# A two-layer hybrid encoder block: layer B's turnings moved from TensorE to VectorE and DRAM, a fourth weight buffer, and a new order of layer B

## The chip, the cores and the metric

The kernel runs on one core of a Trainium2 chip. The metric is the device time of one execution in microseconds. Before the change it is 830.73 us, the median of three runs (830.43 to 831.87).

## What is computed

The input is one sequence of 512 tokens of width 1024, float32. Two layers follow each other, each of the form x + out(mix(norm(x))), with 16 heads of 64 channels.

```python
for i in range(DEPTH):                       # DEPTH = 2
    hn = rms_norm(x, norm_gain[i])
    y = mixer_a(hn, ...) if i % 2 == 0 else mixer_b(hn, ...)
    x = x + y

def mixer_b(hn, w_in, w_out, q_gain, k_gain, rpb):
    q, k, v, gate = split(hn @ w_in, 4)      # 1024 x 4096 weights
    q = rms_norm(q per head, q_gain) * 64 ** -0.5
    k = rms_norm(k per head, k_gain)
    # tokens stand on an 8 x 64 grid; the queries of a block of 16 columns see a slab of
    # 32 columns in all 8 rows, of which 16 columns a query are valid
    p = softmax(q @ k.T + bias)
    y = (p @ v) * silu(gate)
    return y @ w_out                         # 1024 x 1024 weights
```

Layer A (`mixer_a`) has three groups of dilated windows with their own queries, keys and values, merged by their softmax denominators, and takes the first 560 us or so of the trace; layer B is `mixer_b`.

## The kernel before, in words

**Products.** Every product with weights is made of three matmuls: an operand is split into a high part (in the type float32r) and a low part, and high x high, high x low and low x high are added up in PSUM. `mm3` issues the three. A wide product (`project`, line 251) has 512 output columns: for each of 8 slices of the contraction it visits four accumulators (`ps_acc`, four banks), 4 x 8 x 3 = 96 matmuls of 512 columns. A narrow one (`project_t`, line 276: a gate, or layer A's first values) has 24. The output product (`out_product`, line 988) has 8 slices times 8 output tiles times three.

**Weights.** `loads` (line 166) walks the weights in the order in which they are used, in pieces of up to 1024 columns (512 KB). `raws` (line 175) loads a piece on SP's queue into one of three buffers (`wraw`). `split` (line 128) makes the high part on ScalarE (line 132) and the low part (line 138), for two splits in five on GpSimd and for three on VectorE. Four splits are held ahead of TensorE.

**Order.** TensorE's order is the order in which the program is written. `run` (line 954) interleaves two generators: `main`, the products, and `side`, the attention work between them. A clock of estimated TensorE time counts each matmul as it is issued. `later_on` (line 235) puts a job at a later reading of this clock; a `yield "wait", key, delay` in `side` holds until a stamp is set and a delay has passed; a number yielded is a pause. The clock only sets the order of the program: on the chip an instruction waits for its operands. Instructions on the other engines are ordered by a scheduler at build time, but for those marked `keep_in_program_order`. SP's queue works its transfers off in order, and one that waits holds up those behind it.

**Layer B.** `B_PARTS` (line 38) is the order of its products: four wide Q/K products (each for two head pairs), two wide V products, eight gates; then the output product. Behind a Q/K product ScalarE empties each accumulator (line 493), GpSimd squares, VectorE reduces and norms per head (`head_norm`, line 296) and scales (line 313). `side_b(hc)` (line 1072) then handles a head pair: eight 128 x 128 transposes on TensorE (`transpose4`, line 326: four for the queries, four for the keys), copies out of PSUM that split them and bring the tokens into the order of the query blocks (lines 1087 to 1096), 24 score matmuls, a softmax per head and half (line 1131 on VectorE, 1141 and 725 on ScalarE). P^T then comes in one of two ways. For the first six pairs VectorE turns 32 x 32 blocks (`turner.put`, line 795), SP writes them to DRAM (line 804) and reads them back with the blocks exchanged (line 808). For the last two pairs `turn_p` (line 1147) transposes on TensorE, 14 transposes a pair, and VectorE copies them out. `weigh` multiplies with the values, `put_y` (line 727) multiplies with the gate and splits the result. The bias of a pair is read in six small transfers (`bias_b`, line 769). `residual` (line 1030) reads the rows that the output is added to, once all of P is used up.

Layer A moves its queries and keys of six head pairs in the way that the change brings to layer B: blocks of 32 x 32 turned by VectorE (`turn_raw`, line 525), a write to DRAM (line 655) and four reads (line 661).

Of the kernel before, what the change touches and what calls it, by code (L numbers as in the profile page):

```python
# [27 lines left out]
KT = 8  # L28
# [18 lines left out]
def tile_hybrid_encoder(  # L47
# [25 lines left out]

    mid_rc = lambda t: sb(t, 64, [[128, 3], [1, 8], [8, 16]])
    edge_rc = lambda t: sb(t, 0, [[448, 2], [1, 8], [8, 8]])
    mid_q = lambda t: sb(t, 0, [[128, 3], [16, 8], [1, 16]])
    edge_q = lambda t: sb(t, 384, [[64, 2], [8, 8], [1, 8]])
    mid_o = lambda t: sb(t, 64, [[128, 3], [16, 8], [1, 16]])
    edge_o = lambda t: sb(t, 0, [[448, 2], [8, 8], [1, 8]])
    mid_cr = lambda t: sb(t, 64, [[128, 3], [1, 16], [16, 8]])  # L80
    edge_cr = lambda t: sb(t, 0, [[448, 2], [1, 8], [8, 8]])
    mid_n = lambda t: sb(t, 64, [[128, 3], [8, 16], [1, 8]])
    edge_n = lambda t: sb(t, 0, [[448, 2], [8, 8], [1, 8]])

# [14 lines left out]
    gb_d = dr.tile([P, 248], F32, name="gb_d")  # L99

    v0 = [cp.tile([P, 4, P], F32, name=f"v0_{i}") for i in range(2)]
# [39 lines left out]
    def blocks():  # L141
# [10 lines left out]
        yield from outs(A_OUT)  # L152
# [22 lines left out]
    def raws():  # L175
        queue = []
        for src, cols, n in loads():
            raw = wp.tile([P, 1024], F32, tag="wraw", name="wraw", bufs=3)
# [5 lines left out]
            nc.sync.dma_start(dst, src)  # L184
            if behind:
                behind.pop()()
            queue.append((raw, cols, n))
            if len(queue) > 2:
                yield queue.pop(0)
        yield from queue  # L190

    def splits():
        queue = []
# [1176 lines left out]
```

## Time and profile before

| What | us |
|---|---|
| median of three runs | 830.73 |
| the profiled execution | 830.22 |
| its span, first to last instruction | 828.4 |
| TensorE busy | 822.4 |
| VectorE busy | 509.5 |
| ScalarE busy | 431.5 |
| GpSimd busy | 281.7 |

In the rows of the profile PE is TensorE's matmuls and PEld its weight loads, DVE is VectorE, ACT ScalarE, POOL GpSimd, and SPq the queue from which SyncE issues transfers. L215 is a line of the kernel's file; nearly all matmuls have line 215, that of the helper, and are told apart by tile: `acc` is a product, `log` scores, `o` weighing, `tp` a transpose. A row of a group ends with busy time, the mean duration of one in ns, and the idle time ahead of it with what ended it. A row of one line or tile shows the shortest, median and longest duration and the first and last start. A row in order of time begins with start and duration; a bracket is idle time ahead of it. In the row of a stretch each engine's busy time is followed by its count of instructions. Matmuls are pipelined: the distance between two starts, not the duration, is what one costs in a row.

### The profile page before, as it was taken

To read this page: it belongs to the slowest core of one execution; us is meant where nothing else is said; L and a number is where in the kernel's file an instruction comes from. 1 tells how busy PE (TensorE), PEld (TensorE's weight loads), DVE (VectorE), ACT (ScalarE), POOL (GpSimd) and SP (SyncE) were. 2 spreads that over 40 slices of the span, in tenths; PEclk is the share of its full clock that TensorE was granted. 3 is DMA by queue.
4 is the path that set the end of the run, shared out by engine and by line. 5 is a ranking of instruction groups with operands and counts; after the bars stand their busy time and mean duration, and the time that the engine had idled before them with its cause. 6 is when DMAs were issued, how large, how long until landed. Compare 5 with 4: busy or idle time off the path is not lost.

```text
span 828.4 us, 15450 instructions
## 1 busy us (share of the span) xinstructions
PE 822.4 (99%) x5616; PEld 667.2 (81%) x5616; DVE 509.5 (62%) x1356; ACT 431.5 (52%) x905; POOL 281.7 (34%) x424
## 2 busy tenths in 40 slices
PE   9999999999999999999999999999999999999998
PEld 7888888788788788788788787788878877877787
DVE  7374685673673673673684754556565778668653
ACT  7433753654554554553554554444366465774541
POOL 3352443343343343343333152021611625235211
PEclk9999999999999999999999999999999999999999
DMA  7487788779679669669675571373336546456323
GB/s 257 147 234 220 219 217 239 238 219 276 189 203 286 181 203 284 178 196 287 188 211 165 168 207 53 88 262 127 103 104 183 171 130 191 127 158 198 107 95 131
DMA packets 73324, 154.08 MB, mean 186 GB/s; under 512 B 6640, under 2 KB 32368, under 8 KB 73248
## 3 DMA queue, kind: packets, MB, share of 16 engines
q1 hardware_dynamic: 73104, 152.83, 61.8%
q8 instruction: 44, 0.72, 0.4%
q10 hardware_dynamic: 144, 0.26, 0.1%
q14 instruction: 32, 0.26, 0.1%
HBM read 117.04 MB, written 39.04 MB: 188 GB/s over the span
## 4 chain that ended last, share of the span: by engine, by line
PE 94%; ACT 2%; DVE 2%; issue 0%; DMA 0%; DVEq 0%; ACTq 0%
PE acc L215 82%; PE o L215 5%; PE log L215 5%; PE tp L219 2%; ACT p L1141 1%; ACT p L725 1%; DVE hn_l L405 1%; DMA x_all<-in_xt 0%; DVE rawq L313 0%; ACT rawq L493 0%; DVE wl L138 0%; DVE pt L1039 0%; ACT wh L132 0%; DVE p L1131 0%; PE pa L215 0%
## 5 line engine op out<-in xcount | busy, mean ns | idle before, releaser
L132 ACT CAST wh<-wraw 128x512 fp32r<-128x512 f32 (+1 forms) x259 | 158.4, 612 | 273.9 <-PE acc L215 255.5
L215 PE MATMUL acc<-wh,hn_h 128*128 128x512 f32 x704 | 280.0, 398 | 1.2 <-ACT hn_h L404 0.6
L215 PE MATMUL acc<-wh,hn_l 128*128 128x512 f32 x704 | 273.9, 390 | 0.0
L215 PE MATMUL acc<-wl,hn_h 128*128 128x512 f32 x704 | 273.8, 390 | 0.0
L138 POOL TENSOR_TENSOR wl<-wraw,wh 128x512 fp32r<-128x512 f32 (+1 forms) x104 | 136.3, 1311 | 380.3 <-ACT wh L132 364.4
L138 DVE TENSOR_TENSOR wl<-wraw,wh 128x512 fp32r<-128x512 f32 (+1 forms) x156 | 110.5, 709 | 140.9 <-ACT wh L132 140.4
L215 PEld LDWEIGHTS acc<-wh,hn_h 128*128 128x128 f32 x704 | 132.1, 188 | 35.7 <-issue 5.6
L215 PEld LDWEIGHTS acc<-wh,hn_l 128*128 128x128 f32 x704 | 132.2, 188 | 28.3
L215 PEld LDWEIGHTS acc<-wl,hn_h 128*128 128x128 f32 x704 | 132.3, 188 | 25.9 <-POOL wl L138 0.3
L215 PE MATMUL acc<-y,wh 128*128 128x512 f32 (+1 forms) x272 | 82.4, 387 | 0.0
L215 PE MATMUL acc<-hn_h,wh 128*128 128x512 f32 x192 | 76.0, 396 | 0.8 <-ACT rawk L493 0.6
L215 PE MATMUL acc<-hn_h,wl 128*128 128x512 f32 x192 | 74.8, 390 | 0.0
L215 PE MATMUL acc<-hn_l,wh 128*128 128x512 f32 x192 | 74.8, 389 | 0.0
L725 ACT ACTIVATE p<-p,mn 128x512 f32<-128x512 f32 (+3 forms) x128 | 69.6, 585 | 0.6 <-DVE mn L724 0.2
L290 DVE TENSOR_REDUCE ss<-sq 128x4 f32<-128x256 f32 (+1 forms) x96 | 48.4, 504 | 32.8 <-POOL sq L287 22.8
L879 ACT ACTIVATE p<-p,mn 128x512 f32<-128x512 f32 (+1 forms) x64 | 44.9, 702 | 38.9 <-DVE mn L868 38.9
L795 DVE STREAM_TRANSPOSE tr<-p 128x512 f32<-128x512 f32 (+1 forms) x80 | 53.7, 683 | 12.2 <-ACT p L725 10.7
L215 PEld LDWEIGHTS acc<-y,wh 128*128 128x128 f32 x272 | 48.3, 189 | 9.6 <-issue 1.3
L313 DVE TENSOR_TENSOR rawq<-rawq,rs 128x256 f32<-128x256 f32 (+1 forms) x96 | 50.4, 585 | 4.3 <-POOL rs L124 4.0
L215 PE MATMUL acc<-y,wl 128*128 128x512 f32 (+1 forms) x136 | 51.4, 378 | 0.0
L287 POOL TENSOR_TENSOR sq<-rawq 128x256 f32<-128x256 f32 (+1 forms) x48 | 42.2, 891 | 16.3 <-ACT rawq L493 14.5
L289 POOL TENSOR_TENSOR sq<-rawq 128x256 f32<-128x256 f32 (+1 forms) x48 | 34.0, 719 | 34.3 <-ACT rawq L493 27.5
(123 smaller groups left out, 948.7 us busy)
## 6 DMA issues: line engine op xcount, KB each, us to landing
wraw<-in_w SPq DMA_DIRECT2D x119, 512.0 KB
td<-tr SPq DMA_DIRECT2D x14, 1024.0 KB
pt<-td SPq DMA_DIRECT2D x56, 256.0 KB
qd<-rawq SPq DMA_DIRECT2D x6, 1536.0 KB
qt<-qd SPq DMA_DIRECT2D x24, 384.0 KB
td<-tr SPq DMA_DIRECT2D x6, 896.0 KB
pt<-td SPq DMA_DIRECT2D x24, 224.0 KB
e<-l_d SPq DMA_DIRECT2D x32, 112.0 KB
```

The lines of the kernel that those rows point to most:

```text
L132: nc.scalar.copy(h, raw)
L138: eng.tensor_sub(l, raw, h.bitcast(F32))
L215: nc.tensor.matmul(o, l, r, **kw)
L219: nc.tensor.transpose(o, i, ident)
L287: nc.gpsimd.tensor_mul(sq.rearrange("p (f a r) -> p a f r", a=4, r=32), v, v)
L289: nc.gpsimd.tensor_mul(sq, v, v)
L290: nc.vector.tensor_reduce(ss[:, i * ns : (i + 1) * ns], sq.rearrange("p (a b) -> p a b", b=64), axis=AX.X, op=ALU.add)
L313: m = nc.vector.tensor_mul(v, v, by)
L405: return nc.vector.scalar_tensor_tensor(l, xk, g, h.bitcast(F32), op0=ALU.mult, op1=ALU.subtract)
L725: nc.scalar.activation(pr, pr, AF.Copy, scale=mn[:, 3:4])
L795: nc.vector.transpose(dst, src[:, :n].rearrange("p (i b k) -> p i b k", b=4, k=32))
L879: nc.scalar.activation(row, row, AF.Exp, bias=mn[:, 1:2], scale=-1.0, accum_out=mn[:, 2:3])
```

## The change

Layer B's queries and keys of all eight head pairs leave their product in blocks (`blocks_of`, `by_a`), are turned by VectorE, written to DRAM and read back (`move_b`); `side_b` splits them from there, in the order of tokens. P^T of all eight pairs goes by the `turner`. Scores, weighing and the gated result follow the new order of tokens: the query part carries the first 64 tokens once more at its end, and keys are read in four runs of 32 a tile. All low parts of layer B's weights are made by VectorE (`pool[0] = 0`). Loads of weights are issued behind the first half split of the next piece, and in layer B every fourth goes into `v0x`, which layer A has left. The bias of layer B is expanded into full rows in DRAM during layer A. `project` and `out_product` use the fourth accumulator only from the second slice on, with the first two slices held. `B_PARTS` is reordered, and `B_PLAN` sets the clock times, counted from the start of layer B, at which each pair's scores and its weighing are issued. The last two slices of the output product come late, in place of one, and the residual rows are read in two halves.

```diff
 B_PARTS = (
-    ("qk", 0), ("v", 0), ("gate", 0), ("gate", 1), ("qk", 1), ("gate", 2), ("gate", 3),
-    ("qk", 2), ("v", 1), ("qk", 3), ("gate", 4), ("gate", 5), ("gate", 6), ("gate", 7),
+    ("qk", 0), ("v", 0), ("qk", 1), ("gate", 0), ("gate", 1), ("gate", 2), ("qk", 2), ("gate", 3), ("gate", 4), ("qk", 3), ("v", 1), ("gate", 5), ("gate", 6), ("gate", 7),
 )
 B_OUT = B_IN + 4 * KT * D
+B_PLAN = (
+    ("scores", 0, 47700), ("scores", 1, 70000), ("values", 0, 82000), ("scores", 2, 87000),
+    ("values", 1, 108000), ("scores", 3, 108700), ("values", 2, 117000), ("scores", 4, 125400),
+    ("scores", 5, 145000), ("values", 3, 145000), ("scores", 6, 165000), ("values", 4, 166000),
+    ("scores", 7, 176700), ("values", 5, 180000), ("values", 6, 198000), ("values", 7, 213000),
+)
 W_COLS = B_OUT + KT * D
...
+    v0x = cp.tile([P, 1024], F32, name="v0x")
+    v0 = [v0x[:, 512 * i : 512 * i + 512].rearrange("p (i c) -> p i c", i=4) for i in range(2)]
...
-        yield from outs(A_OUT)
+        yield from outs(A_OUT, 1)
         b = B_IN
         for kind, _ in B_PARTS:
             n = P if kind == "gate" else 512
             yield b, n, KT
             b += n * KT
-        yield from outs(B_OUT)
-
-    def outs(b):
-
-        for n, ks in ((512, KT - 1), (384, KT - 1), (512, 1), (384, 1), (128, KT)):
+        yield from outs(B_OUT, 2)
+
+    def outs(b, late):
+
+        k = KT - late
+        for n, ks in ((512, k), (384, k)) + ((512, 1), (384, 1)) * late + ((128, KT),):
             yield b, n, ks
             b += n * ks
...
+    in_b = [False]
+
+    def splits():
+        ahead, queue, src = [], [], loads()
+        count = [0]
+
+        def load():
+            piece, cols, n = next(src, (None, 0, 0))
+            if not cols:
+                return
+            count[0] += in_b[0]
+            if in_b[0] and count[0] % 4 == 1:
+                raw = v0x
+            else:
+                raw = wp.tile([P, 1024], F32, tag="wraw", name="wraw", bufs=3)
             dst = raw[:, :cols]
             if not begun:
-                nc.scalar.dma_start(dst[:, :n], src[:, :n])
+                nc.scalar.dma_start(dst[:, :n], piece[:, :n])
                 begun.append(load_x(1, 2))
-                dst, src = dst[:, n:], src[:, n:]
-            nc.sync.dma_start(dst, src)
+                dst, piece = dst[:, n:], piece[:, n:]
+            m = nc.sync.dma_start(dst, piece)
+            if in_b[0]:
+                tc.keep_in_program_order(m)
             if behind:
                 behind.pop()()
-            queue.append((raw, cols, n))
-            if len(queue) > 2:
-                yield queue.pop(0)
-        yield from queue
-
-    def splits():
-        queue = []
-        for raw, cols, n in raws():
+            ahead.append((raw, cols, n))
+
+        late = False
+        for _ in range(3):
+            load()
+        while ahead:
+            raw, cols, n = ahead.pop(0)
             step = 384 if n == 384 else 512
             for c in range(0, cols, step):
                 queue.append((*split(raw[:, c : c + step], step), min(n, step)))
+                if late and not c:
+                    load()
                 if len(queue) > 3:
                     yield queue.pop(0)
+            late = True
...
+            if k < 2 and not need:
+                held.append((h, l))
+                for i in range(3):
+                    mm3(acc[i][:, :n], stat_h(k, i), stat_l(k, i), h, l, k == 0, False)
+                    yield
+                for j, (h, l) in enumerate(held if k else ()):
+                    mm3(acc[3][:, :n], stat_h(j, 3), stat_l(j, 3), h, l, j == 0, False)
+                    yield
+                continue
...
+        def spread_out(rows, cols, first, n, src, o):
+            dst = bass.AP(
+                eb_d.tensor, eb_d.offset + rows * 16 * 384 + first * 384 + cols, [[16 * 384, 32], [384, n], [1, src[1]]]
+            )
+            t, width = src[0], src[0].shape[1]
+            tc.keep_in_program_order(
+                nc.sync.dma_start(
+                    dst, bass.AP(t.tensor, t.offset + rows * width + o, [[width, 32], [-8, n], [1, src[1]]])
+                )
+            )
+
+        for n, r in enumerate(range(0, P, 32)):
+            later_on(30000 + 40000 * n, partial(spread_out, r, 0, 0, 16, (lb_d, 256), 120))
+            later_on(45000 + 40000 * n, partial(spread_out, r, 256, 0, 8, (gb_d, P), 56))
+            later_on(55000 + 40000 * n, partial(spread_out, r, 256, 8, 8, (gb_d, P), 120))
...
+    vv = wk.tile([P, 1024], F32, tag="vt", name="vv", bufs=1)
+    FS = {"rawq": (6, 0, 4), "rawk": (6, 4, 6), "raw": (4, 0, 4), "raw0": (4, 0, 2), "raw1": (4, 2, 4)}
+
+    def blocks_of(i, key, order="p (a f) r -> p a f r", **kw):
+        fs, f0, f1 = FS[key]
+        x = rq[:, : 512 * fs].rearrange("p (c i r) -> p c i r", i=4, r=32)[:, :, i, :]
+        x = x.rearrange(order, f=fs, **kw)
+        return x[:, f0:f1] if kw else x[:, :, f0:f1]
...
+            move = [partial(move_b, 2 * hc + f) for f in range(2)]
+            head_norm("raw0", ss, 4, 0, True, then=move[0])
+            head_norm("raw1", ss2, 4, 18000, then=move[1])
             for n in range(2):
-                st[key, 2 * hc + n] = raw[:, :, 256 * n : 256 * n + 256]
                 stamp[key, 2 * hc + n] = clock[0]
...
+    def move_b(hc):
+
+        x = by_a("raw%d" % (hc % 2))
+        for a in (0, 2):
+            nc.vector.transpose(x[:, a : a + 2], x[:, a : a + 2])
+        d = dr.tile([4, P, 256], F32, name="bd", tag="bd", bufs=2)
+        place, left = (vv if hc % 2 else rq[:, 2048:3072]).rearrange("p (t f x) -> p t f x", t=4, f=2), [4]
+
+        def write():
+            tc.keep_in_program_order(nc.sync.dma_start(d.rearrange("a p x -> p a x"), x))
+            stamp["qk", hc] = 0
+
+        def read(a):
+            dst = place[32 * a : 32 * a + 32].rearrange("k t f x -> k t (f x)")
+            src = d[a].rearrange("(t k) x -> k t x", t=4)
+            tc.keep_in_program_order(nc.sync.dma_start(dst, src))
+            left[0] -= 1
+
+        out, back = (6000, 13500) if hc % 2 else (14000, 20500)
+        later_on(out, write)
+        for a in (0, 2, 1, 3):
+            later_on(back, partial(read, a))
+        st["raw", hc] = place, left
...
-            for grid, line in ((mid_rc, mid_o), (edge_rc, edge_o)):
-                nc.vector.tensor_mul(grid(gt), grid(gt), line(o))
+            nc.vector.tensor_mul(gt, gt, o)
...
-            r0 = (2 * hc + hd) * 8
-            nc.sync.dma_start(
-                e[:, hd, 0:256],
-                bass.AP(lb_d.tensor, lb_d.offset + r0 * 376 + 120, [[376, 8], [-8, 16], [1, 256]]),
-            )
-            for i, st in enumerate((120, 56)):
-                nc.sync.dma_start(
-                    e[64 * i : 64 * i + 64, hd, 256:384],
-                    bass.AP(gb_d.tensor, gb_d.offset + r0 * 248 + st, [[248, 8], [-8, 8], [1, P]]),
-                )
+            m = nc.sync.dma_start(e[:, hd, :], eb_d[2 * hc + hd].rearrange("(r c) x -> c r x", r=8))
+            tc.keep_in_program_order(m)
...
+                if not self.left:
+                    stamp["back", self.key] = clock[0]
...
+            if k < 2:
+                held.append(next(wsteps))
+                yield from step(k, range(3), held[k])
+                for j in range(2 * k):
+                    yield from step(j, (3,), held[j])
+                continue
...
+        yield ("yb", hc - 5, "y") if hc else ("rs", "all")
+        if hc in (3, 4):
...
-        tp = transpose4(raw, 0)
-        for src, dst in ((mid_rc(tp), mid_q(qh)), (edge_rc(tp), edge_q(qh))):
-            nc.scalar.copy(dst, src)
-        for src, h, l in (
-            (mid_rc(tp), mid_q(qh), mid_q(ql)),
-            (edge_rc(tp), edge_q(qh), edge_q(ql)),
-        ):
-            nc.vector.tensor_sub(l, src, h.bitcast(F32))
-        yield 2500 if hc < NHC - 1 else 2000
-        tp = transpose4(raw, P)
-        scaled(kh, tp, 3)
-        nc.vector.scalar_tensor_tensor(kl, tp, gk[:, 3:4], kh.bitcast(F32), op0=ALU.mult, op1=ALU.subtract)
-        stamp["qk", hc] = 0
-        yield 1750 if hc < NHC - 1 else 1250
+        landed, left = raw
+        assert not left[0]
+        qk = wk.tile([P, 2 * EXT + 2 * S], F32R, tag="q12", name="qkb", bufs=1)
+        qh, ql = qk[:, :EXT], qk[:, EXT : 2 * EXT]
+        kh, kl = (qk[:, 2 * EXT + S * n : 2 * EXT + S * n + S].rearrange("p (t x) -> p t x", t=4) for n in range(2))
+        tokens = lambda t: t[:, :S].rearrange("p (i t r) -> p t i r", i=4, t=4)
+        src = lambda f: landed[:, :, f, :]
+        q_src = src(0).rearrange("p t (i r) -> p t i r", i=4)
+        first = lambda t: t[:, S:EXT].rearrange("p (t r) -> p t r", t=2)
+        tc.keep_in_program_order(nc.scalar.copy(tokens(qh), q_src))
+        tc.keep_in_program_order(nc.scalar.copy(first(qh), landed[:, 0:2, 0, 0:32]))
+        tc.keep_in_program_order(nc.vector.tensor_sub(tokens(ql), q_src, tokens(qh.bitcast(F32))))
+        nc.gpsimd.tensor_copy(ql[:, S:EXT], ql.bitcast(F32)[:, 0:64])
+        yield 700
+        tc.keep_in_program_order(scaled(kh, src(1), 3))
+        m = nc.vector.scalar_tensor_tensor(kl, src(1), gk[:, 3:4], kh.bitcast(F32), op0=ALU.mult, op1=ALU.subtract)
+        tc.keep_in_program_order(m)
+        yield 3800
...
+                i0, step = (b, 1) if b < 3 else (0, 3)
+                m = lambda t_, hs: sb(t_[hs], 32 * i0, [[32 * step, 2], [P, 4], [1, 32]])
+                qs = slice(64 + P * b, 192 + P * b)
...
-                normalise(pr[:, o : o + n], mn)
+            sums = mns.rearrange("p (b x) -> p b x", b=2)
+            nc.vector.reciprocal(sums[:, :, 3:4], sums[:, :, 2:3])
+            for o, n, c in ((0, 256, 3), (256, 256 if u == 0 else P, 7)):
+                nc.scalar.activation(pr[:, o : o + n], pr[:, o : o + n], AF.Copy, scale=mns[:, c : c + 1])
             return pr
-
-        def turn_p(hd, u, pr):
-            tp = bank("tp")
-            n = 4 if u == 0 else 3
-            for i in range(n):
-                transpose(tp[:, i * P : (i + 1) * P], pr[:, i * P : (i + 1) * P])
-            dst = sb(pt, at(0, hd, 4 * u), [[32, n], [448, 4], [1, 32]])
-            nc.vector.tensor_copy(dst, tp[:, : n * P].rearrange("p (i a r) -> p i a r", i=n, a=4))
...
+        turned = turner(448, hc)
+        turners.append(turned)
+        for hd, u, pr in held:
+            turned.put(pr, 512 if u == 0 else 384, 224 * hd + 128 * u)
+        ready, back, pace = 7500, 7500, 500
+        later_on(ready, partial(turned.send, pt[:, :1792], back, pace))
+        pending.append(lambda: put_y(hc, weigh(), False, hc == NHC - 1))
...
+        in_b[0] = True
+        pool[0] = 0
+        stamp["b", "start"] = clock[0]
...
-            yield from side_b(hc)
-        yield from residual(xm_d)
-        stamp["yb", KT - 1, "y"] = 0
+        for job, hc, delay in B_PLAN:
+            yield "wait", ("b", "start"), delay
+            if job == "scores":
+                yield from side_b(hc)
+                continue
+            yield "wait", ("back", hc), 3500
+            if hc == NHC - 2:
+                stamp["yb", "turned"] = 0
+            pending.pop(0)()
+            yield
+            if hc >= NHC - 2:
+                yield from residual(xm_d, 4 * (hc % 2))
```

More of the change, by code (lines that the diff above doesn't have):

```diff
@@ L292, in squares, with head_norm @@
         )
-    later = []
-    def head_norm(raw, ss, ns, held, delay=0, quick=False, then=None):
+    def head_norm(raw, ss, ns, delay=0, quick=False, then=None):
         rs = wk.tile([P, 32], F32, tag="rs", name="rs")
@@ L317, in scale @@
                 then()
-        if held:
-            later.append(scale)
-        elif delay:
+        if delay:
             later_on(delay, scale)
@@ L465, in project_qk @@
         box = []
-        blocked = moved(hc) and key in FS
+        blocked = key == "raw" or (moved(hc) and key in FS)
         def evac(i, acc):
@@ L1004, in out_product @@
             acc[f] = ps_acc.tile([P, 512], F32, tag="acc", name="acc")
-        for k in range(KT - 1):
+        held = []
+        for k in range(KT - late):
             chore(True)
             yield key, k, "y"
+            if k < 2:
[4 more added lines that the diff above has]
+                continue
             yield from step(k, range(4))
@@ L1011, in out_product @@
             acc[f] = bank("acc2")
-        for k in range(KT - 1):
+        for k in range(KT - late):
             yield from step(k, range(4, 7))
-        yield key, KT - 1, "y"
-        yield from step(KT - 1, range(4))
-        yield from step(KT - 1, range(4, 7))
+        for k in range(KT - late, KT):
+            yield key, k, "y"
+            yield from step(k, range(4))
+            yield from step(k, range(4, 7))
         acc[7] = ps_acc.tile([P, 512], F32, tag="acc", name="acc")
@@ L1254, in side @@
                 yield from attn_a(hc)
-        yield from residual(xg)
+        yield from residual(xg, 0)
+        yield from residual(xg, 4)
         stamp["ya", KT - 1, "y"] = 0
```

139 lines of the change are left out of this document (47 added, 92 removed).

## The prediction

> **What bounds the kernel now.** I read the page first, then stretches of time, groups by line, the chain, and TensorE's own order of time.
>
> ```profile
> span 828.4 us, 15450 instructions
> ...
> PE 822.4 (99%) x5616; PEld 667.2 (81%) x5616; DVE 509.5 (62%) x1356; ACT 431.5 (52%) x905; POOL 281.7 (34%) x424
> ...
> PE 94%; ACT 2%; DVE 2%; issue 0%; DMA 0%; DVEq 0%; ACTq 0%
> ```
>
> TensorE is busy in 822.4 of 828.4 us and is 94% of the chain that ended last. The profiled run took 830.22 us, so 1.8 us lie outside its span; it is 0.5 us under the median of the runs (830.73). About 0.2% (1.7 us) is what a measurement of this kernel can tell from no change.
>
> ```profile
> core 0: us, PE busy (x) PEld busy (x) DVE busy (x) ACT busy (x) POOL busy (x), PEclk, DMA share, GB/s
> 579.00:800.00 221.00, 219.71 (x1256) 175.04 (x1255) 150.47 (x466) 125.83 (x321) 79.32 (x121) 1.00 0.47 140
> ```
>
> This stretch is most of layer B, which starts near 560 us. TensorE has almost no air in it, VectorE is at 68%, ScalarE at 57%, the DMA engines at about half. So only two things shorten the run: matmuls that go, and pauses between matmuls.
>
> **The change, part by part.** First, the transposes of layer B on TensorE: two groups in the same stretch, and the chain shows their price on the path.
>
> ```profile
> L215 PE MATMUL log<-qkb 64*128 64x256 f32 x192 | 13.8, 289 | 0.0
> ...
> L219 PE MATMUL tp<-ident,rawq 128*128 128x128 f32 x64 | 9.6, 272 | 0.0
> L215 PE MATMUL o<-pt,rawk 128*64 128x256 f32 x64 | 9.2, 380 | 0.0
> ...
> L219 PE MATMUL tp<-ident,p 128*128 128x128 f32 x28 | 4.5, 276 | 0.1
> ...
> 597.50 0.44 PE tp L219 x4
> 597.93 2.77 PE acc L215 x12
> ```
>
> The mean of one (272 ns) overlaps its neighbours; the chain's 0.44 us for a block of four is what the path pays, 0.11 each. There are 64 for queries and keys and 28 for P^T of the last two head pairs: 92 x 0.11 = **10.1 us, all gone**. Nothing on TensorE takes their place: scores keep 24 matmuls a pair, weighing 12.
>
> Second, pauses. Neighbours in TensorE's order of time:
>
> ```profile
> 562.12 0.39 PE L215 MATMUL acc<-wh,hn_l 128*128 128x512 f32 x1
> 562.68 0.50 PE L215 MATMUL acc<-wh,hn_h 128*128 128x512 f32 x1 [0.17 <-DVE pt L1039]
> ...
> 608.77 0.39 PE L215 MATMUL acc<-wh,hn_l 128*128 128x512 f32 x1
> 609.81 0.50 PE L215 MATMUL acc<-hn_h,wh 128*128 128x512 f32 x1 [0.65 <-ACT rawk L493]
> 610.15 0.39 PE L215 MATMUL acc<-hn_l,wh 128*128 128x512 f32 x1
> ...
> 690.13 0.40 PE L215 MATMUL acc<-wh,hn_l 128*128 128x512 f32 x1
> 690.82 0.50 PE L215 MATMUL acc<-wh,hn_h 128*128 128x512 f32 x1 [0.29 <-ACT rawq L493]
> ```
>
> Matmuls in a row start 0.23 us apart (2.77 / 12). The three gaps are 0.56, 1.04 and 0.69 us, so 0.33 + 0.81 + 0.46 = 1.6 us are lost, and each first matmul then takes 0.34 us to the next (609.81 to 610.15) in place of 0.23: 0.3 us more. Together 1.9 us. Each is a product that waits for its accumulator to be emptied, behind softmax work on ScalarE or norms on VectorE. The change meets them twice: the fourth accumulator of a wide product is first used behind 18 matmuls, not 9 (2 us later), and the plan by head pair places the softmaxes apart from the ends of products (scores 0 now come after the first V product). The gain is between 0 (the first three accumulators are used as early as before) and 1.9. I take 1.9, because two of the three waits have such a place in the new order; what is late next is the landing below.
>
> Third, what is added on VectorE and taken from GpSimd:
>
> ```profile
> L138 DVE TENSOR_TENSOR wl<-wraw,wh x39: 549/691/1782, 582.6 to 795.9; 128x512 fp32r<-128x512 f32 x37, 128x384 fp32r<-128x384 f32 x2
> ...
> L138 POOL TENSOR_TENSOR wl<-wraw,wh x26: 1012/1290/1465, 579.8 to 790.5; 128x512 fp32r<-128x512 f32 x25, 128x384 fp32r<-128x384 f32 x1
> ...
> L750 DVE TENSOR_TENSOR gt<-gt,o 128x384 f32<-128x384 f32 (+1 forms) x15 | 9.7, 694 | 7.1 <-PE o L215 6.9
> L724 DVE RECIPROCAL mn<-mn 128x1 f32<-128x1 f32 x64 | 8.7, 154 | 8.4 <-ACT p L1141 7.7
> ...
> L530 DVE STREAM_TRANSPOSE rawq<-rawq x24: 662/956/1237, 49.4 to 375.1; 128x512 f32<-128x512 f32 x12, 128x1024 f32<-128x1024 f32 x12
> ```
>
> The 26 low-part subtractions of GpSimd come to VectorE: 26 x 0.69 = 18 us. Sixteen transposes of 512 columns at the short form's 0.66 us are 10.6 us. P^T of two more pairs replaces as many copies from PSUM and nets to about nothing. The multiplication by the gate becomes one instruction for two (about -5), reciprocals halve (-4.4). Net +19: VectorE goes from 150 to about 169 us, and the stretch shrinks by some 11 us to 210: 80%. That is under TensorE, so its cost on the path is zero as long as the four splits held ahead (4 x 2.77 = 11 us of matmuls) cover each VectorE batch; without that cover each us of lateness is a us of the run.
>
> [...]
>
> Fourth, the way through DRAM. Each pair's turned queries and keys are one write of 512 KB and four reads of 128 KB on SP's queue. The nearest rows are layer A's 1536 KB trip and its first consumer on ScalarE:
>
> ```profile
> 67.86 0.38 SPq L655 DMA_DIRECT2D qd<-rawq  x1
> 69.14 0.33 SPq L184 DMA_DIRECT2D wraw<-in_w  x1
> 74.12 1.75 SPq L661 DMA_DIRECT2D qt<-qd  x4
> 75.98 4.72 SPq L184 DMA_DIRECT2D wraw<-in_w  x2
> 80.75 0.43 SPq L574 DMA_DIRECT2D vd<-vx  x1
> ...
> L698 ACT ACTIVATE k<-qt,gk x6: 1183/1284/1339, 85.1 to 393.6; 128x512 f32<-128x512 f32 x6
> ...
>   DMA qt<-qd: 1.7, 1
> ```
>
> Write to first read: 6.3 us. First read to landing: 11.0 us (74.12 to 85.1, the consumer having waited 1.7 us for it). Up to 1536 + 1024 + 256 KB moved in it, about 262 GB/s. A pair of layer B (512 KB of reads beside one 512 KB weight load) then lands in about 4.0 us, an estimate; bounds 2.0 (the reads alone at that rate) and 11.0. Ahead of the score matmuls lie then two ScalarE copies, a scaled copy and a VectorE operation; their forms of before:
>
> ```profile
> L1087 ACT CAST qkb<-tp x16: 268/368/481, 598.0 to 781.1; 128x384 fp32r<-128x384 f32 x8, 128x128 fp32r<-128x128 f32 x8
> L1092 DVE TENSOR_TENSOR qkb<-tp,qkb x16: 274/412/559, 598.7 to 781.9; 128x384 fp32r<-128x384 f32 x8, 128x128 fp32r<-128x128 f32 x8
> L698 ACT ACTIVATE qkb<-tp,gk x8: 671/688/689, 601.2 to 783.4; 128x512 fp32r<-128x512 f32 x8
> L1096 DVE SCALAR_TENSOR_TENSOR qkb<-tp,gk,qkb x8: 749/750/751, 601.9 to 784.2; 128x512 fp32r<-128x512 f32 x8
> ```
>
> 2 x 0.37 + 0.69 + 0.75 = 2.2 us, with hand-overs 2.4. What the plan leaves I count in the kernel's own clock (20.5 us a wide product, 5.1 a gate, the plan's times): the reads of pairs 0, 2, 4 and 6 go out 5.7, 2.9, 1.4 and 4.8 us ahead of their score step, those of odd pairs over 5, and the matmuls come 4.5 us behind the step's start. That clock has 0.213 us for a matmul that takes 0.231, so times 1.08. The room for landing is 8.6, 5.6, 4.0 and 7.6 us. At 4.0 us only pair 4 is at its edge. Behind ScalarE's copy, which is pinned, stand weight casts, and TensorE has 11 us of splits before it feels those. I take **+1.5 us**. P^T has over 5 us behind its last read everywhere in the plan, so nothing is charged; the last residual rows go out some 7 us ahead of their use.
>
> Fifth, at nothing: the bias rows, twelve transfers in layer A of 3.1 MB in all (12 us at 262 GB/s, spread over more than 150 us), and each weight load issued half a split later (2.8 us); both eat into a lead of three loads, 16 us of matmuls, and would cost what they overrun it by. In layer B two bias reads a pair stand for six, and the fourth weight buffer lets loads go out without waiting.
>
> **Sum**: 828.4 - 10.1 - 1.9 + 1.5 = 817.9 us of span, plus 1.8 outside: **819.7 us**.
>
> **Rivals.** *Landing becomes the wait* (slower). Place: the score steps of pairs 0, 2, 4, 6. If every landing took layer A's 11.0 us, they would be 2.4, 5.4, 7.0 and 3.4 us late, 18.2 in all: 819.7 - 1.5 + 18.2 = **836.4 us**. It decides from a landing of about 9.5 us, where 0.9 + 3.9 + 5.5 + 1.9 = 12.2 eats the gain. For it: one queue carries all, weight loads too. Against: a third of the bytes, and a DMA share of 0.47.
>
> *VectorE becomes the bound* (no change). Place: after each of the four wide Q/K products, where reduces, the norm, scalings and now transposes meet all subtractions. If TensorE lost a split (2.8 us) there each time, that is 11 us: **831 us**. It decides when a VectorE batch holds a subtraction up for over 11 us. Against: 80% busy. For it: subtractions that range from 549 to 1782 ns. [...]
>
> *Pauses stay and a few landings are later*: no 1.9 us, and up to 4 us more: 821.6 to 825.6, taken as **824 us**. For it: ScalarE carries the softmaxes as before.
>
> *The change doesn't do what it says*: the scores now read keys in runs of 32 columns, and TensorE gives back what it saved. If each of the 96 steps (192 / 2) went from the 289 ns of the row above to the 380 of weighing, which reads such runs, that is 8.7 us: **828.4 us**. Against: weighing works on plain float32, which alone can be the difference.
>
> **How the numbers follow.** Forecast 0.58 (816 to 822), pauses stay 0.19, scores dearer 0.05, VectorE 0.06, landing 0.12. Faster: 0.58 + 0.19 + 0.05 = 0.82; same 0.06; slower 0.12. The range begins at 815.5 (no late landing gives 818.2, and pauses too small to be in the three gaps may go too) and ends at 827, where the last three cases, mostly, are left out.
>
> **What would show it.** No transposes between 579 us and the end; the scores of pairs 2 and 4 either start 0.23 us behind their neighbour (right) or behind a DMA of the landed tile (rival); pauses at the starts of products under 0.2 us; VectorE near 80% in layer B; matmuls of the scores still near 289 ns. I am wrong if TensorE's idle time in layer B grows past 5 us, or if layer A, up to 555 us, moves by over 1 us.

## The result and the profile after

| | before | after |
|---|---|---|
| median, us | 831.3 (830.43 to 831.99, 4 runs) | 816.38 (816.17 to 816.63, 4 runs) |
| ratio | | 0.9821, 95% interval 0.9804 to 0.9838 |
| the profiled execution, us | 830.22 | 816.17 |
| last weighing of layer A starts, us | 532.10 | 531.97 |
| from there to the end of the span, us | 296.30 | 282.43 |

The change is faster by 1.8%, and 3.3 us below the forecast of 819.7, inside its range. The last two rows of the table split the span at one instruction of the chain, `532.10 3.62 PE o L215 x48` before and `531.97 3.62 PE o L226 x48` after. Layer A stayed as it was; layer B became 13.87 us shorter. The experiments below are compared by this stretch (called layer B from here on), because in 8 of the 14 profiled executions 1.6 to 2.4 us are lost at the very start, where the first products begin 0.43 to 0.47 us apart in place of some 0.25, and by their times two of the four runs of before in the table have this loss and none of after. A second profile of the changed kernel (e9_again, below) gave 282.40.

The page of the changed kernel, the lines that answer to those of before: span, busy times, the chain by engine.

```profile
span 814.4 us, 15249 instructions
...
PE 808.9 (99%) x5524; PEld 659.0 (81%) x5524; DVE 526.8 (65%) x1356; ACT 430.5 (53%) x905; POOL 245.9 (30%) x400
...
PE 94%; DVE 3%; ACT 2%; DMA 0%; issue 0%; POOL 0%; DVEq 0%
```

TensorE is still busy in all but 5.5 us, with 92 instructions fewer (5616 to 5524): these are the transposes. The stretches of layer B, each engine's busy time with its count, then the granted clock, the DMA share and GB/s:

```profile
core 0: us, PE busy (x) PEld busy (x) DVE busy (x) ACT busy (x) POOL busy (x), PEclk, DMA share, GB/s
565.00:786.00 221.00, 220.46 (x1216) 178.54 (x1215) 168.65 (x481) 132.90 (x334) 51.70 (x103) 1.00 0.68 201
680.00:720.00 40.00, 39.46 (x221) 31.53 (x220) 35.92 (x104) 26.02 (x72) 12.00 (x26) 1.00 0.72 207
```

TensorE's air in 221 us shrank to 0.54 us. VectorE is at 76% of the whole but at 90% (35.92 of 40) from 680 to 720 us, and that is where the only two waits of TensorE in layer B lie. TensorE's waits (us in total, times, longest), and its order of time around both:

```profile
PE acc L226 <- ACT rawq L530: 0.4, 1, 0.4
PE log L226 <- DVE qkb L1153: 0.2, 1, 0.2
```

```profile
702.71 0.39 PE L226 MATMUL acc<-wh,hn_l 128*128 128x512 f32 x1
703.03 0.39 PE L226 MATMUL log<-qkb 64*128 64x256 f32 x2
703.59 1.59 PE L226 MATMUL log<-qkb 64*128 64x256 f32 x22 [0.18 <-DVE qkb L1153]
705.11 0.50 PE L226 MATMUL acc<-wh,hn_h 128*128 128x512 f32 x1
...
713.20 0.39 PE L226 MATMUL acc<-wh,hn_l 128*128 128x512 f32 x1
713.95 0.50 PE L226 MATMUL acc<-wh,hn_h 128*128 128x512 f32 x1 [0.36 <-ACT rawq L530]
```

The scores of pair 4 take 703.03 to 705.11, 2.08 us, where a block without a wait takes 1.63, as this one of the chain does, so 0.45 us are lost:

```profile
761.83 1.63 PE log L226 x22
```

The pause at 713.95 is 0.75 us between starts in place of 0.23: 0.52 lost. What the scores waited for is told by the rows below: VectorE's queue, GpSimd's instruction beside it, ScalarE's two copies for this pair and the issue of its reads, each in order of time, and the landing of all such reads:

```profile
698.62 1.53 DVE L133 TENSOR_TENSOR wl<-wraw,wh 128x512 fp32r<-128x512 f32 x1
700.07 0.68 DVE L1149 TENSOR_TENSOR qkb<-rawq,qkb 128x512 fp32r<-128x512 f32 x1
700.67 0.41 DVE L778 SCALAR_TENSOR_TENSOR gx<-eg,gx 128x256 f32<-128x256 f32 x1
701.01 1.29 DVE L716 STREAM_TRANSPOSE rawq<-rawq 128x512 f32<-128x512 f32 x2
702.23 0.65 DVE L133 TENSOR_TENSOR wl<-v0x,wh 128x512 fp32r<-128x512 f32 x1
702.80 0.74 DVE L1153 SCALAR_TENSOR_TENSOR qkb<-rawq,gk,qkb 128x512 fp32r<-128x512 f32 x1
```

```profile
698.30 1.30 POOL L811 TENSOR_TENSOR y<-gt,y 128x512 fp32r<-128x512 f32 x1 [10.71 <-ACT y L810]
```

```profile
697.08 0.63 ACT L1147 CAST qkb<-rawq 128x512 fp32r<-128x512 f32 x1
698.79 0.73 ACT L758 ACTIVATE qkb<-rawq,gk 128x512 fp32r<-128x512 f32 x1
```

```profile
690.56 1.74 SPq L727 DMA_DIRECT2D rawq<-bd  x4
```

```profile
DMA to landing us min/median/max: 2.3/3.8/7.3
```

Reads go out from 690.56 on, ScalarE copies at 697.08 with no DMA wait ahead of it. The key's high part is there at 699.52, but its low part (L1153) starts only at 702.80, behind two low parts of weights and the next pair's turnings: VectorE's queue was late, the landing was not. The first of these low parts took 1.53 us, where the middle of its group is 0.69; it ran beside the GpSimd multiplication shown, and the 0.84 us more are above the 0.45 that the scores lost. That the scores would not have waited without it is argued, not shown.

### The profile page after: what moved, and what is told of

Read it like the earlier page. It is cut to its first block, busy times and chain, and to the rows that moved or that the text cites. A ratio compares the mean times of both kernels' runs of the same rounds, so it can differ in the third digit from the quotient of the medians.

```text
span 814.4 us, 15249 instructions
## 1 busy us (share of the span) xinstructions
PE 808.9 (99%) x5524; PEld 659.0 (81%) x5524; DVE 526.8 (65%) x1356; ACT 430.5 (53%) x905; POOL 245.9 (30%) x400
## 4 chain that ended last, share of the span: by engine, by line
PE 94%; DVE 3%; ACT 2%; DMA 0%; issue 0%; POOL 0%; DVEq 0%
PE acc L226 82%; PE log L226 5%; PE o L226 5%; PE tp L230 1%; ACT p L1197 1%; DVE wl L133 1%; ACT p L1203 1%; DMA x_all<-in_xt 0%; DVE rawq L330 0%; ACT rawq L530 0%; DVE rawq L716 0%; PE pa L226 0%; POOL sq L308 0%; PE pk L226 0%; DVE ss L311 0%
## 5 line engine op out<-in xcount | busy, mean ns | idle before, releaser
L226 PE MATMUL acc<-wh,hn_h 128*128 128x512 f32 x704 | 278.4, 396 | 1.2 <-ACT hn_h L419 0.8
L226 PE MATMUL acc<-wl,hn_h 128*128 128x512 f32 x704 | 274.0, 390 | 0.0
L226 PE MATMUL acc<-wh,hn_l 128*128 128x512 f32 x704 | 273.8, 390 | 0.0
L127 ACT CAST wh<-wraw 128x512 fp32r<-128x512 f32 (+1 forms) x240 | 146.3, 613 | 218.2 <-PE acc L226 199.4
L133 DVE TENSOR_TENSOR wl<-wraw,wh 128x512 fp32r<-128x512 f32 (+1 forms) x169 | 119.9, 712 | 128.4 <-ACT wh L127 128.3
L133 POOL TENSOR_TENSOR wl<-wraw,wh 128x512 fp32r<-128x512 f32 (+1 forms) x72 | 94.5, 1312 | 249.3 <-ACT wh L127 231.7
L226 PEld LDWEIGHTS acc<-wh,hn_h 128*128 128x128 f32 x704 | 132.1, 188 | 34.3 <-issue 5.4
L226 PEld LDWEIGHTS acc<-wh,hn_l 128*128 128x128 f32 x704 | 132.2, 188 | 27.9
L226 PEld LDWEIGHTS acc<-wl,hn_h 128*128 128x128 f32 x704 | 132.3, 188 | 26.2 <-POOL wl L133 0.2
L308 POOL TENSOR_TENSOR sq<-rawq 128x256 f32<-128x256 f32 (+1 forms) x80 | 63.5, 806 | 87.1 <-ACT rawq L530 76.2
L226 PE MATMUL acc<-y,wh 128*128 128x512 f32 (+1 forms) x272 | 81.6, 384 | 0.0
L226 PE MATMUL acc<-hn_h,wh 128*128 128x512 f32 x192 | 75.5, 393 | 0.0
L226 PE MATMUL acc<-hn_l,wh 128*128 128x512 f32 x192 | 74.8, 390 | 0.0
L226 PE MATMUL acc<-hn_h,wl 128*128 128x512 f32 x192 | 74.8, 389 | 0.0
L846 DVE STREAM_TRANSPOSE tr<-p 128x512 f32<-128x512 f32 (+1 forms) x88 | 58.3, 678 | 19.7 <-ACT p L1203 9.1
L932 ACT ACTIVATE p<-p,mn 128x512 f32<-128x512 f32 (+1 forms) x64 | 44.9, 703 | 42.3 <-DVE mn L921 42.3
L226 PEld LDWEIGHTS acc<-y,wh 128*128 128x128 f32 x272 | 48.8, 189 | 10.1 <-issue 1.3
L226 PE MATMUL acc<-y,wl 128*128 128x512 f32 (+1 forms) x136 | 51.3, 378 | 0.0
L530 ACT ACTIVATE rawq<-acc,rs_n 128x512 f32<-128x512 f32 (+1 forms) x76 | 44.6, 612 | 0.6
L785 ACT ACTIVATE p<-p,mn 128x512 f32<-128x512 f32 (+1 forms) x64 | 43.4, 698 | 0.4 <-DVE mn L784 0.4
```

Source lines behind the costliest of these rows:

```text
L127: nc.scalar.copy(h, raw)
L133: eng.tensor_sub(l, raw, h.bitcast(F32))
L226: nc.tensor.matmul(o, l, r, **kw)
L308: nc.gpsimd.tensor_mul(sq.rearrange("p (f a r) -> p a f r", a=4, r=32), v, v)
L530: nc.scalar.activation(dst, src, AF.Copy, scale=rs_n[:, i : i + 1])
L785: nc.scalar.activation(pr, pr, AF.Copy, scale=mn[:, 3:4])
```

## The experiments

All experiments compute the whole of the reference; the transposes added in the first two are results that nothing reads.

**What a transpose costs** (e1_tp4 and e2_tp1): sixteen blocks put back into layer B, at about the two places of a pair where they stood, of four transposes and of one.

```diff
+        def idle():
+            tp = bank("tp")
+            for i in range(4):   # 1 in e2_tp1
+                nc.tensor.transpose(tp[:, i * P : (i + 1) * P], ident, ident)
+        idle()
         yield 700
...
-        yield 3800
+        yield 1900
+        idle()
+        yield 1900
```

> The changed kernel with 64 idle transposes put back on TensorE: in each head pair's score step two blocks of four, of the identity matrix, whose result nobody reads; the kernel's clock doesn't count them, so all else keeps its place. Theory (the price on the path is that of the chain's rows, 0.44 us a block): 16 blocks cost 7.0 us, 823.4 us. Second theory (a block also leaves a slow stretch behind it, since the path fell by 3.5 us more than the sum said): 7.9 us or more, 824.3 us. Rival (TensorE has slack there): under 1 us, 816.4 to 817.4.

> The same with blocks of one in place of four: 16 transposes in 16 places. If the price goes by the number of transposes (0.11 us each), 1.8 us: 818.2 us. If it goes by the break between two kinds of matmul, about 0.25 us a place, 4 us: 820.4 us.

Medians 824.37 and 819.93; layer B 289.60 and 284.11, so +7.17 us for 64 transposes and +1.68 for 16, 0.112 and 0.105 us each. Both are somewhat less than the transposes cost, because TensorE waits less in these runs: the scores of pair 4 take 1.62 and 1.63 us in place of 2.08, and the pause behind them is 0.41 and 0.43 in place of 0.52. With that put back it is 7.74 and 2.22 us, which makes 0.115 us a transpose and 0.023 for the break of a block in the row of products. So the price goes by the number of transposes in the main, and the 92 removed ones, in 24 blocks, were worth 10.3 us by the plain difference and about 11.2 by the corrected one.

**What the hold of the fourth accumulator is worth** (e3_no_hold: the changed kernel without it; e4_before_hold: the kernel before with it).

```diff
-            if k < 2 and not need:
+            if False:
```

> The changed kernel with the wide products in their old order: the fourth accumulator is used from the first slice on (the output products keep the new order). If the held slices are what removed pauses, the pauses at the starts of wide products return, 0.3 to 1.5 us: 816.7 to 818. If the new places of the softmaxes removed them, no change: 816.4 us, and no pause over 0.2 us at the start of a wide product.

Median 817.88, layer B 283.0 (+0.57). One pause came back, 0.32 us at 562.77; the scores of pair 4 took 2.17 in place of 2.08. The pauses at 609 and 742 us of before did not return, so other parts of the change had removed these. The new order is the likely one, but no run has it alone.

```diff
+            if k < 2 and not need:
+                held.append((h, l))
+                for i in range(3):
+                    mm3(acc[i][:, :n], stat_h(k, i), stat_l(k, i), h, l, k == 0, False)
+                    yield
+                for j, (h, l) in enumerate(held if k else ()):
+                    mm3(acc[3][:, :n], stat_h(j, 3), stat_l(j, 3), h, l, j == 0, False)
+                    yield
+                continue
```

> The kernel before with only the held slices of the wide products added. Theory (only a wait for the fourth accumulator can be met this way): the pause at 562 us goes, 0.4 us, and those at 609 and 690 us stay: 830.5 to 831. Rival (the hold alone removes the pauses): all of them, 1.9 us: 829.3 us.

Median 834.82, ratio to before 1.0047 (1.003 to 1.0064): slower, layer B +3.46 us, which neither theory had. TensorE's order of time, and a stretch, of e4:

```profile
572.49 0.39 PE L215 MATMUL acc<-wh,hn_l 128*128 128x512 f32 x1
575.47 1.02 PE L215 MATMUL pk<-ones,ssq 128*128 128x1 f32 x8 [2.60 <-DVE ssq L1061]
...
578.31 0.63 PE L215 MATMUL acc<-wh,hn_l 128*128 128x512 f32 x1
578.73 0.63 PE L215 MATMUL acc<-wh,hn_h 128*128 128x512 f32 x1
```

```profile
576.00:581.00 5.00, 5.00 (x18) 4.02 (x18) 2.41 (x12) 0.62 (x1) 0.00 (x0) 0.66 0.16 35
```

The hold takes the pause at 562 away and puts a worse wait in its place: the row sums of the norm, issued at a set point of the product's order, now come up before VectorE has the sum of the squares, which itself ends 2.7 us later than before (both counted from layer A's last weighing), after a wait of 2.01 us for a square from ScalarE. 2.98 us lie between the two starts, 2.75 more than in a row. Behind it matmuls start 0.43 us apart, not 0.23, at a granted clock of 0.66: about 1.5 us more. So e10_before_hold_late_sums issues the row sums later:

```diff
-        yield 2600
+        yield 4500
```

> The kernel before with the held slices and, as in the changed one, the row sums of layer B 1.9 us later on the kernel's clock (4500 for 2600). Theory (the hold alone brought TensorE to the row sums 2.75 us ahead of VectorE's sum, and its clock fell behind that wait): the wait and the slow matmuls go, the pause at 562 us stays away, 830.0 to 830.3 us by the layer-B part, 0.4 us better than before. Rival (the held order itself costs): still 833 or more.

Median 832.03, ratio 1.0004 (0.9994 to 1.0015); layer B 296.11, 0.2 us below before. No slow matmuls are left, and the wait for the sums fell to 0.75 us, which takes most of what two pauses gave (0.33 and 0.46). The pause of 0.8 us ahead of the first V product stays. The hold alone gains nothing that the times can tell.

**Whether VectorE is the next bound** (e5_dve3: each turning of queries and keys done three times, +21 us on VectorE; an odd number gives the same result).

```diff
-            nc.vector.transpose(x[:, a : a + 2], x[:, a : a + 2])
+            for _ in range(3):
+                nc.vector.transpose(x[:, a : a + 2], x[:, a : a + 2])
```

> The changed kernel with each turning of queries and keys done three times on VectorE (three times gives the same as once): 32 more transposes of 512 columns, 21 us more VectorE work in layer B, 75% to about 85% of it over all and near 100% in its busiest 40 us. If VectorE still is cover there, no change: under 0.5 us, 816.4 to 816.9. If VectorE is the next bound, as the 0.45 us lost at the scores of pair 4 hints, TensorE waits for scores and low parts: 2 to 10 us more, 818 to 826.

Median 824.29, layer B 288.34: +5.9 us. TensorE's waits of e5, those that after has none or little of:

```profile
PE log L226 <- DVE mns L1188: 2.4, 1, 2.4
PE log L226 <- DVE qkb L1154: 2.1, 1, 2.1
PE acc L226 <- ACT rawq L530: 1.6, 1, 1.6
```

Of the 21 us more, 5.9 came through: at the scores of pairs 2 and 4, and at the pause that after already has. The other 15 us were covered. VectorE is what TensorE waits for next.

**Whether VectorE can be relieved** (e6_pool1: one low part in five on GpSimd).

```diff
-        pool[0] = 0
+        pool[0] = 1
```

> The changed kernel with GpSimd again making one low part in five of layer B: some 13 subtractions fewer on VectorE (9 us), at 1.3 us each on GpSimd. If VectorE's load causes the last pauses (0.5 us ahead of gate 5 and 0.45 us in the scores of pair 4), they shrink: 815.4 to 816.2. If it doesn't, no change: 816.4. If a low part from GpSimd comes too late, a loss: over 817.

Median 818.56, layer B 283.18 (+0.75): no gain. The scores of pair 4 took 2.62 us, half a us more, and the last pause stayed at 0.56. This does not speak against VectorE as the cause of these waits, because VectorE was hardly relieved: 16 low parts fewer in layer B, 9 us of work, made it only 1.4 us less busy (198.2 to 196.8). Other instructions of it took longer, here the low part of the queries for four pairs (the mean is the second figure behind the bar), first in after and then in e6:

```profile
L1149 DVE TENSOR_TENSOR qkb<-rawq,qkb 128x512 fp32r<-128x512 f32 x4 | 2.7, 682 | 0.0
```

```profile
L1149 DVE TENSOR_TENSOR qkb<-rawq,qkb 128x512 fp32r<-128x512 f32 x4 | 4.2, 1060 | 0.6 <-ACT qkb L1147 0.6
```

All 25 VectorE instructions of layer B that took over 0.2 us more than the middle of their kind in e6 ran beside a GpSimd instruction, and so did all 11 in after and all 18 in before. Summed over all that ran beside one, VectorE took 14.5, 6.7 and 10.5 us more than by these middles.

**What the way through DRAM costs** (e7_reads2: each read issued twice; e11_bytes2: 512 KB more a pair, copied to a place that nothing reads).

```diff
-            tc.keep_in_program_order(nc.sync.dma_start(dst, src))
+            for _ in range(2):
+                tc.keep_in_program_order(nc.sync.dma_start(dst, src))
```

> The changed kernel with the four reads of each pair's turned queries and keys issued twice, the same bytes to the same place: 512 KB more a pair, and a landing later by 2 us (512 KB at 262 GB/s) or more. Theory (room for landing is 4 us or more and it lands in 3.1): within 0.5 us, 816 to 816.9. Rival (landing is the next wait): 1 to 2 us for each of pairs 2 and 4 and for weights behind them in the queue, 818 to 820.

Median 849.01, ratio to before 1.0216 (1.0199 to 1.0234); layer B 314.23, +31.8. SyncE's queue and TensorE's waits of e7:

```profile
647.95 12.47 SPq L728 DMA_DIRECT2D rawq<-bd  x8
...
665.46 14.99 SPq L728 DMA_DIRECT2D vv<-bd  x8
```

```profile
PE log L226 <- ACT qkb L759: 13.1, 4, 6.1
PE o L226 <- DMA pt<-td: 7.1, 1, 7.1
```

SyncE's own waits, for an earlier read into the same place:

```profile
SPq L728 <- DMA vv<-bd: 39.3, 16, 6.2
SPq L728 <- DMA rawq<-bd: 32.8, 16, 3.5
```

This was no test of bytes. The second read of a place waits for the first, four reads that took 1.74 us to issue became eight in 12.47, and all else on that queue stood behind them. What it shows is the mechanism of the landing rival at its price: reads that take over 12 us to go out, scores waiting up to 6.1 us, a run slower than before. e11 doubles a pair's bytes without such a wait:

```diff
+        d2 = dr.tile([4, P, 256], F32, name="bd2", tag="bd2", bufs=2)
...
             tc.keep_in_program_order(nc.sync.dma_start(dst, src))
+            tc.keep_in_program_order(nc.sync.dma_start(d2[a], d[a]))
```

> The changed kernel with, behind each of the four reads of a pair, a copy of the same 128 KB from DRAM to another place in DRAM: 512 KB more read and written a pair and four more entries on SP's queue, with nothing waiting for them. If bytes decide the landing: 512 KB at 262 GB/s is 2 us later, still within the room of 4 us and more, so under 0.5 us: layer B 282.4 to 283. If queue slots decide: under 0.5 us as well. If landing is near the edge after all: 1 us or more at the scores of pairs 2 and 4, layer B over 284.

Median 818.49, layer B 282.79 (+0.37). All of it lies behind the last matmul (3.85 us to the end of the span, where after has 3.48); the scores of pair 4 took 2.07 us (2.08 in after), though the last of its reads went out 3.2 us behind the first, in place of 1.3. The landing is not the edge: neither bytes nor places in the queue decide, at this size.

**Whether the fourth weight buffer is free** (e8_buf3: layer B with three).

```diff
-            if in_b[0] and count[0] % 4 == 1:
+            if False:
```

> The changed kernel without the fourth weight buffer: layer B's loads go through three buffers as in layer A. Theory (the buffer only spares SP's queue some waiting, which nothing on the path feels): no change, 816 to 816.9. Rival (loads that wait hold up the DRAM trips behind them by up to a split's time, 2.8 us): late scores, 817.5 to 821.

Median 818.82, layer B 283.74 (+1.31). TensorE's order of time in e8, at the weighing of pair 6:

```profile
779.20 0.39 PE L226 MATMUL acc<-y,wl 128*128 128x512 f32 x1
780.85 1.50 PE L226 MATMUL o<-pt,rawk 128*64 128x128 f32 x19 [1.26 <-DMA pt<-td]
```

Without the buffer a weight load holds SyncE's queue until a low part frees its place (from 560 us on 103.1 us of such waits against 28.9 in after). The reads of this pair's P^T go out at 773.05, behind two such loads, where after has 763.02, and TensorE starts the weighing 1.3 us late.

**The changed kernel again, and one pair more** (e9_again; e12_one_more_moved: layer A's seventh pair, of which the change leaves the transposes on TensorE, turned and moved too).

> The changed kernel itself, once more beside the others. The layer-A part of the runs so far ended at 532 us in some and at 534 us in others, the 2 us being lost in the first 11 us. If that is chance at the start, this kernel shows it too, 816.2 to 818.6 us, and its layer B (from the last weighing of layer A to the end of the span) stays at 282.4 us within 0.3; then 0.6 us (no hold), 0.75 (GpSimd) and 1.3 (three buffers) are real losses of those kernels. If layer B itself wanders by 1 us, they are not.

Median 816.54, layer B 282.40.

```diff
-    moved = lambda hc: hc < NHC - 2
+    moved = lambda hc: hc < NHC - 1
...
-            yield "wait", ("rawk", hc + 1), 0
+            yield "wait", ("rawk" if hc < NHC - 2 else "rawq", hc + 1), 0
```

> The changed kernel with layer A's seventh head pair moved through DRAM as well: its six blocks of transposes on TensorE go (24 transposes), VectorE turns its queries and keys. At 0.11 us a transpose 2.7 us: layer A's last weighing ends 2.7 us sooner, 813.7 us (816 with the slow start). If a wait takes their place (the seventh pair's reads or its P^T land late, since the eighth pair follows in another order), the gain is under 1 us or turns into a loss of some us.

Median 819.25, 2.9 us above the changed kernel. Layer B is as it was (282.37); layer A, from its row sums to its last weighing, is 2.1 us longer. TensorE's order of time in e12:

```profile
457.75 0.59 PE L226 MATMUL log<-k,qt 64*32 64x256 f32 x2
460.60 0.45 PE L226 MATMUL log<-k,qt 64*32 64x256 f32 x7 [2.26 <-DVE gt L806]
...
462.79 0.63 PE L226 MATMUL acc<-wh,hn_l 128*128 128x512 f32 x1
463.22 0.63 PE L226 MATMUL acc<-wh,hn_h 128*128 128x512 f32 x1
```

The transposes are gone there too, but the scores, which now come sooner, find their accumulator not yet emptied by VectorE (`gt`, a wait of 2.26 us), and matmuls 0.43 us apart follow, in place of 0.23. No version of these beats the changed kernel.

## Why the prediction was right, step by step

**Transposes**, 10.1 us: right in kind, about 1 us too small. A transpose cost 0.115 us and the break of a block 0.023 (e1, e2), about 11.2 in all; the 0.44 us of the chain leave out that the next six products, too, start a little later. In the place of the 64 for queries and keys VectorE has sixteen turnings, 10.4 us, beside which TensorE lost 0.97 us in two waits (the step on VectorE, below).

**Pauses**, 1.9 us: the sign right, the size too small, and one of the two causes overrated. Neighbours before show 2.58 us in seven gaps, where I counted three (0.33, 0.81 and 0.46; the others are 0.26, 0.15, 0.35 and 0.22), after 0.52 in one; with the longer first matmul behind each the gain is about 2.6 us. The hold did little of it: without it 0.57 us came back (e3), and in the kernel before it gained 0.2 at best (e10). That the plan did the rest is likely, not shown. That the wait goes elsewhere when the hold moves TensorE ahead (e4) was a price that I had not seen; the changed kernel, with its later row sums, has no such wait.

**VectorE at no cost**, 169 us: the size about right (168.65 us in a stretch of 221, 76%, where I had 169 in 210, 80%), and the cover of 11 us held except around pair 4 and the pause behind it, where VectorE is busy 90% of the time. The mean over the stretch hid this. The chain of waits after says the same: it leaves TensorE at 670.97 and comes back at 713.95.

```profile
662.57 8.38 PE acc L226 x36
670.97 2.74 ACT rawq L530 x4
...
702.88 0.66 DVE qkb L1153
...
713.31 0.59 ACT rawq L530
713.95 11.85 PE acc L226 x51
```

For 43 us VectorE and ScalarE follow on each other almost without air; TensorE lost 0.97 us in that time (0.45 and 0.52).

**DRAM trip**, +1.5 us: wrong in its cause. I had pair 4 "at its edge" for the landing. Landings took 2.3 to 7.3 us, 3.8 in the middle (I took 4.0), and no score waited for one. Pair 4 did lose 0.45 us, behind VectorE. This term was 1.0 us too much, and the price belongs to the step on VectorE. Twice the bytes changed 0.37 (e11), none of it at the scores.

**At nothing**: bias rows and later loads, right as far as layer A goes (0.13 us shorter). The fourth weight buffer is not a thing at nothing: without it 1.31 us are lost (e8), so the change needs it to come out at its price.

The sum by what was measured: 11.2 + 2.6 - 0.45 = 13.35 of the 13.87 us. Another 0.25 is that the scores of the last two pairs took 1.75 us each before, where the others took 1.62 (1.63 after). Products in a row also follow each other closer, 0.2282 us apart in the mean over 944 before and 0.2270 over 1004 after, 1.1 us; half of that lies in the six products behind each block of transposes and is in their price, and why the rest is so stays open. The forecast had about 10.5 us less than the profiled run of before: the transposes, the pauses and the DRAM trip were all off to the same side, by 1.1, 0.7 and 1.0 us, so the time came out 0.9 us above the lower end of the range. That landings would not be late and that smaller pauses would go too is what the lower end had been set for; that the transposes' price, off to the same side, did not carry the time out of the range was luck.

**The rivals.** *Landing becomes the wait*: did not happen. That it can make the run slower than before, e7 shows (849.01 us, where I had 836.4 for landings of 11 us), but there the queue was held by waits, and bytes alone did not do it (e11). *VectorE becomes the bound*: not at 169 us, in part at 190 (e5). The work that left GpSimd (busy for 79.32 us of a stretch of 221 before, 51.70 after) counts here too: in instructions that ran beside one of GpSimd, VectorE took 10.5 us more in layer B before than by the middles of their kinds, 6.7 after, and 14.5 when e6 gave some work back. The medians of the low parts hide it (691 ns before, 689 after); it sits in single instructions of up to 1782 ns before and 1528 after. The traces show the two side by side, not what holds them. *Pauses stay*: one of 0.52 us did. *Scores dearer*: no. The group of the scores after, busy time and mean of one:

```profile
L226 PE MATMUL log<-qkb 64*128 64x256 f32 x192 | 13.9, 289 | 0.2 <-DVE qkb L1153 0.2
```

289 ns as before: runs of 32 columns cost nothing here.

## What to carry to other kernels

Where one engine is busy 99% of the run, its instructions are priced by the distance between starts in a row (here 0.115 us a transpose, which itself takes 0.272), and moving one of them to an engine with air is worth that price, as long as the receiving engine is looked at by stage and not by its mean: here 76% over layer B was 90% where the only losses lay. What a third engine does at the same time counts as well: 9 us of work given back to GpSimd freed VectorE by 1.4 us. A wait is moved more easily than removed: the same hold cost 3.46 us in the kernel before and gained 0.57 in the changed one, so after each such edit the next instruction with a wait has to be looked for. A second transfer to the same place, or a load that waited for its buffer, held up what was queued behind it, which cost 31.8 us in e7 and 1.31 in e8, where twice the bytes alone cost 0.37.

## What the hardware showed beside

Some waits of TensorE cost more than themselves here. Behind waits of 2.60 us (e4), 2.26 (e12) and 2.33 (one of e7's, with 0.69 more shortly after it) the products started 0.43 us apart, in place of 0.23, for 2.7 to 3.7 us (462.37 to 464.50 and a little on both sides in e12). The granted clock was 0.66 from 576 to 581 us in e4 and 0.64 from 462 to 466 us in e12. This adds 1.2 to 1.6 us. Length alone does not decide it: waits of 2.37 and 2.15 us in e5 were followed by products 0.23 us apart, as TensorE's order of time in e5 shows for the longer one:

```profile
666.85 0.98 PE L226 MATMUL log<-qkb 64*128 64x256 f32 x11 [2.37 <-DVE mns L1188]
...
668.32 0.40 PE L226 MATMUL acc<-wh,hn_l 128*128 128x512 f32 x1
668.56 0.39 PE L226 MATMUL acc<-wh,hn_h 128*128 128x512 f32 x1
```

The granted clock stayed at 1.00 there, from 668 to 671 us and, behind the wait of 2.15 us, from 711 to 715. Why e4, e7 and e12 have slow products behind a wait of this length and e5 has none is not shown.
